# Two layers of a hybrid diffusion backbone: the scan's output split inside the scan's own program, responses in quarters of the TensorE array, rounding on ScalarE and merged rotations

## The chip, the cores and the metric

One core of one Trainium2 chip runs the whole program in one launch. The metric is device microseconds from the first to the last instruction, with what lies around them, as the median of several executions. Engine names are those of the profile: PE (TensorE matrix products), PEld (its weight loads), DVE (VectorE), ACT (ScalarE), POOL (GpSimd), SP (SyncE, whose only work here is issuing DMAs).

## What is computed

Input is a 1024-token latent stream and a 256-token context, both 1024 wide. Layer 0 runs two gated linear recurrences. Layer 1 runs windowed attention with 16 query heads and, beside it, an S5 state-space mixer; its output is what this case is about. All of it is computed in float32. The S5 half of layer 1, cut from the reference:

```python
for direction in range(2):
    abar = jnp.exp(lam * dt)
    bbar = ((abar - 1.0) / lam)[:, :, None] * bmat
    st_c = diag_scan(abar, order(einsum('blgh,gph->lbgp', uc, bbar)), None)
    st_l = order(diag_scan(abar, order(einsum('blgh,gph->lbgp', ul, bbar)), st_c[-1]))
    y_l = y_l + real(einsum('lbgp,ghp->blgh', st_l, cmat))
z = gelu(y_l)                      # then GLU: (z @ Wa) * sigmoid(z @ Wb) * silu(g_s5)
```

There are 64 channel groups of 16 channels, each with one complex diagonal state of size 64 in each direction.

## The kernel before

**Precision.** A matrix product in float32 accuracy is three products of fp32r halves: `mm3` (L67) issues high by high (L69), high by low (L70), low by high (L71). `split` (L63) makes the halves: the high one is a copy on ACT (L64), the low one a subtraction on DVE (L65). Small products of the S5 part run directly in f32; the trace shows each as two instructions. A f32 transpose is one.

**Layer 1 first stage (`layer1`, L904).** `main` (L932) projects the normed activations: eight units `u` (the S5 input), two `v`, two `k`, then 24 units `ga`, `gs`, `q`. A unit is one 128-column weight block (`g_fm`, L148): for each chunk of 512 tokens 24 matmuls into one of two PSUM banks, then an evacuation. That is 88 steps (yields) of `main`. `gs` units are passed through Silu (`silu`, L884) and stored to `gsD` (L971) in order of time.

**The scans' program (`S5.run`, L1427)** is a second generator that `weave` (L42) advances beside `main`: after step i of `main`, side steps are emitted until they stand in the ratio ns:nm to i (L975: 109 side steps to 83 main steps). It computes parameters (`params`, 11 steps), builds matrices for 16 groups-of-four (`build_a` L1469, `build_b` L1498) and runs 32 pairs of groups, three steps each:

- `table` (L1532): the rotation angles of a pair are rounded with two additions of a large constant (L1546, L1547, L1551, all DVE), then Sin on ACT (L1553, L1555). The scan's decays `dec` are written by ACT (L1545).
- `front_a` (L1561): input product on PE (L1576), evacuated on ACT to `sd`.
- `front_b` (L1585): rotate by the table (two products L1592, a subtraction L1593, an addition L1594), scan (L1595), rotate back (two products L1598, L1600, L1601), copy to `sx` (L1603, L1604 on ACT).
- `back` (L1606): output product on PE (L1614, L1616); after every fourth pair Gelu, and a store to `zF` (L1622).

In `build_a` the short responses are 8 products with a 128x128 block `g` as weights and 32 columns `kc` moving (L1490).

The tile framework takes the program's order as a priority and fixes each engine's queue when the kernel is built; within an engine, instructions then run in that order, each waiting for its inputs. SP's DMA queue is one such order: a DMA that waits for a buffer holds up those behind it. When a pool of tiles is closed, its memory goes to later pools, whose tiles wait for the last use of what lay there.

**The second stage.** After the weave, `g_glu` (L1029) loads z: for each of 8 channel blocks `cb`, eight loads into one of two buffers `zr` (L1037), then two splits (L1041) that turn the scans' order (t, n) into order of time (position 8n + 7 - t) with stride-8 access. Its tiles lie in the memory of pools that are closed after the weave. Then 16 units `b` and `a` of the GLU over two chunks of z (mm<-zh, whi), with `gsD` read back (L1053) and the result stored to `yT1` (L1056). `g_out` (L825) then multiplies this half by the output weights, adds the residual rows `x1` and stores partial rows `x2p` (`part`, L999). All of this is `main` (L989), woven with attention (`g_att`, L1072; scores L1131, softmax L1140 to L1151, products L1162 to L1171) at 46:150. The final `g_out` (L1025) does the attention half, block by block, reading `x2p`.

Of the kernel before, what the change touches and what calls it, by code (L numbers as in the profile page):

```python
# [9 lines left out]
F32 = mybir.dt.float32  # L10
# [8 lines left out]
D = 1024  # L19
# [35 lines left out]
class Body:  # L55
# [848 lines left out]
    def layer1(self):  # L904
# [8 lines left out]
        gaD = dram.tile([8, 128, 1024], F32, name="gaD")  # L913
        gsD = dram.tile([8, 128, 1024], F32, name="gsD")
        zF = dram.tile([64, 8, 16, 128], F32, name="zF")
# [12 lines left out]
        with tc.tile_pool(name="psum1", bufs=1, space=PSUM, reuse_waits="tile") as ps5:  # L928
            s5 = S5(self, left, ps5, uF, zF)
            nu = [0]  # L930

            def main():  # L932
# [28 lines left out]
                for kind, i in oB:  # L961
                    def ev(ps, c0, n):
                        lc = slice(c0 - 256, c0 - 256 + n)
                        if kind == "q":
                            self.rope(ps, c0, n, 0.125, [
                                qD[lc.start // 128:lc.stop // 128, i // 2, a * 32:a * 32 + 32,
                                   i % 2 * 2 + h].rearrange("b d t -> d b t")
                                for a in range(2) for h in range(2)])
                        else:
                            t = self.silu(ps, n)  # L970
                            self.nc.scalar.dma_start((gaD if kind == "ga" else gsD)[i, :, lc], t)  # L971
# [4 lines left out]
        left.close()  # L976
        self.right.close()
# [5 lines left out]
        with ExitStack() as low:  # L983
# [5 lines left out]
            def main():  # L989
                with tc.tile_pool(name="w1c", bufs=1, reuse_waits="tile") as wp, \  # L990
                        tc.tile_pool(name="zt", bufs=1, reuse_waits="tile") as zp:
                    st.end = len(st.order)
                    st.rawp, st.where = wp, lambda j: w1p if j % 2 == 0 else wp
                    yield from self.g_glu(zp, wp, zF, gsD)
                w1.close()
# [6 lines left out]
                yield from self.g_out(A["wo1"], self.yT1, 8, lat, lambda b: self.gl,  # L1002
                                      lambda b: self.x1[b * 128:b * 128 + 128], part, wp, b0=2, late=self.G)

# [23 lines left out]

    def g_glu(self, zp, wp, zF, gsD):  # L1029
        nc, V, S = self.nc, self.V, self.S  # L1030
        hz = [[zp.tile([128, 8, 512], F32R, name=f"z{x}{c}") for x in "hl"] + [c * 512, 512] for c in range(2)]
        st = self.st
        st.load(st.i + 1)
        for cb in range(8):
            t = zp.tile([128, 8, 128], F32, name="zr", tag="zr", bufs=2)
            for g in range(8):
                nc.sync.dma_start(t[g * 16:g * 16 + 16], zF[cb * 8 + g].rearrange("t h n -> h t n"))  # L1037
            t = t[:, ::-1].rearrange("p t n -> p n t")
            for zh, zl, c0, n in hz:
                h, lo = (x[:, cb].rearrange("p (n t) -> p n t", t=8) for x in (zh, zl))  # L1040
                self.split(h, lo, t[:, c0 // 8:(c0 + n) // 8])  # L1041
        yield
        for i in range(8):
            tb = {}

            def ev_b(ps, c0, n):
                t = tb[c0] = wp.tile([128, 512], F32, name="tb", tag="tb", bufs=3)
                S.activation(t, ps, AF.Tanh, scale=0.5)  # L1048

            def ev_a(ps, c0, n):  # L1050
                t = tb[c0]
                g = wp.tile([128, 512], F32, name="gsl", tag="gsl", bufs=2)
                nc.sync.dma_start(g, gsD[i, :, c0:c0 + n])  # L1053
# [192 lines left out]
class S5:  # L1246


    def __init__(self, K, left, ps, uF, zF):
        self.K, self.A, self.nc, self.left = K, K.A, K.nc, left  # L1250
        self.V, self.S, self.G, self.T = K.V, K.S, K.G, K.T
# [28 lines left out]
    def params(self):  # L1280
# [10 lines left out]
        self.exp(dt, raw[:, 2], n, r)  # L1291
        yield
        tt(wr, lre, dt, op=OP.mult)
# [53 lines left out]
        for t in range(2, 9):  # L1347
# [6 lines left out]
            tt(pw[:, 1, :, t], a, b, op=OP.add)  # L1354
        yield
        blk = self.wt("s5blk", (128, 16, 512), 1)
# [20 lines left out]
        stt(phl, dt, i2, phl, op0=OP.mult, op1=OP.add)  # L1377
        yield
        for x, y in ((wh, i1), (wh, i2), (dt, i1)):
# [29 lines left out]
        tt(out(0), out(0), t1, op=OP.subtract)  # L1409
        yield  # L1410
# [4 lines left out]
        yield  # L1415
        tt(out(4), cr, col(5), op=OP.mult)
# [10 lines left out]
    def run(self, nu):  # L1427

        nc, left, tile_pool = self.nc, self.left, self.K.tc.tile_pool
        par = left.enter_context(tile_pool(name="s5p", bufs=1, reuse_waits="tile"))  # L1430
        self.k5 = par.tile([128, 8, 64], F32, name="s5k5")
        self.nidx = par.tile([128, 320], F32, name="nidx")
        nc.sync.dma_start(self.nidx, self.A["nidx"])
# [18 lines left out]
        for p in range(32):  # L1452
# [11 lines left out]
            yield  # L1464
        self.back(todo.pop(0))

    steps = 11 + 2 + 96

    def build_a(self, c):  # L1469
# [23 lines left out]
        pv = pk[:, :128].rearrange("p (g d h) -> p d g h", g=4, d=2)  # L1493
        S.activation(kf[:, 1], pv[:, 1], AF.Copy)
# [37 lines left out]
    def table(self, p):  # L1532

        V, S = self.V, self.S
        ts, stt = V.tensor_scalar, V.scalar_tensor_tensor
        n, mask = self.nidx[:, :160], self.nidx[:, 160:]

# [6 lines left out]
        for g in range(2):  # L1544
            S.activation(dec[:, g], mask[:, None, :].to_broadcast([128, 2, 160]), AF.Copy, scale=col(2, g))  # L1545
# [39 lines left out]
    def front_b(self, q):  # L1585
# [3 lines left out]
        tab, dec = self.tabs.pop(q.p)  # L1589
        R, Q = self.wt("sr", (128, 2, 2, 160), 1), self.wt("sq", (128, 2, 2, 160), 2)  # L1590
        for o, i in ((R, 0), (Q, 1)):
            tt(o, q.D[:, i][:, :, None, :].to_broadcast([128, 2, 2, 160]), tab, op=OP.mult)  # L1592
        tt(R[:, :, 0], R[:, :, 0], Q[:, :, 1], op=OP.subtract)  # L1593
        tt(R[:, :, 1], R[:, :, 1], Q[:, :, 0], op=OP.add)  # L1594
        V.tensor_tensor_scan(*(x.rearrange("p a b n -> p (a b n)") for x in (Q, dec, R)), 0.0, op0=OP.mult, op1=OP.add)  # L1595
        U, W = R[:, :, :, 0:128], self.wt("sw", (128, 2, 2, 128), 1)
        for o, i in ((U, 0), (W, 1)):
            tt(o, Q[:, :, i, 31:159][:, :, None, :].to_broadcast([128, 2, 2, 128]), tab[:, :, :, 32:160], op=OP.mult)  # L1598
        Y = Q[:, :, :, 0:128]
        tt(Y[:, :, 0], U[:, :, 0], W[:, :, 1], op=OP.add)  # L1600
        tt(Y[:, :, 1], W[:, :, 0], U[:, :, 1], op=OP.subtract)  # L1601
        q.x = self.wt("sx", (128, 2, 2, 128), 3)
        S.activation(q.x[0:64], Y[0:64], AF.Copy)  # L1603
        S.activation(q.x[64:128], Y[64:128, :, :, ::-1], AF.Copy)  # L1604

# [48 lines left out]
def s5_host(f, A):  # L1654
# [17 lines left out]
    A["s5d"] = d  # L1672
    A["nidx"] = np.broadcast_to(np.concatenate([np.arange(160), np.arange(160) > 0]), (128, 320)).astype(np.float32)
    sh = np.zeros((128, 128), np.float32)
# [90 lines left out]
```

## Time and profile before

| what | value |
|---|---|
| median of 3 runs | 2752.55 us (2750.77 to 2753.32) |
| the profiled execution, its own time | 2755.79 us |
| its span, first to last instruction | 2754.0 us |
| mean granted clock of TensorE | 0.986 of full |
| busy: PE, PEld, DVE, ACT, POOL | 97%, 84%, 69%, 50%, 17% of the span |

Matmuls overlap, so PE's busy time is not its rate; the rate is read from the starts of successive matmuls in the timeline. A wait is put down to the engine whose instruction ended last before it. In the windows, "x57" counts instructions that run in a stretch, also those that only reach into it.

### The profile page before, as it was taken

The numbers are of one execution on the slowest core, as the hardware profiler recorded it, in microseconds if no ns is written. First come the engines' busy times: TensorE is split into PE (matmuls) and PEld (weight loads), VectorE is DVE, ScalarE is ACT, GpSimd is POOL, SyncE is SP. The second block draws the span as 40 slices with busy tenths as digits, with TensorE's granted clock in tenths as the row PEclk, the third lists the DMA queues.
The fourth block names the chain that finished last, engine by engine and source line by source line (L and its number), as shares of the span: only waits on it lengthen the run. The fifth ranks groups of instructions, "written<-read, shape, count | busy, mean of one in ns | idle before, by whom it ended". The sixth has DMA issues, their size and how long they took to land. (4 is left out here: it accounts for less than half of the span.)

```text
span 2754.0 us, 44850 instructions
## 1 busy us (share of the span) xinstructions
PE 2663.5 (97%) x15664; PEld 2300.3 (84%) x15664; DVE 1912.0 (69%) x5052; ACT 1381.4 (50%) x2907; POOL 456.9 (17%) x817
## 2 busy tenths in 40 slices
PE   6999999999999999998999999999999899999998
PEld 4998989888898888887887789888888688878887
DVE  5556655554565646637467679999996588899886
ACT  5545545434445435437233215666666455576552
POOL 1121120212212222223000000000000022225420
PEclk9999999999999999999999999999999899999999
DMA  6101011111110111123463445344443633243423
GB/s 241 33 24 60 26 49 41 49 54 51 56 57 31 57 56 41 53 65 108 134 208 127 161 129 127 101 133 108 117 110 115 178 89 107 89 146 121 133 97 128
DMA packets 231396, 262.24 MB, mean 95 GB/s; under 512 B 71105, under 2 KB 173761, under 8 KB 230913
## 3 DMA queue, kind: packets, MB, share of 16 engines
q1 hardware_dynamic: 178464, 223.97, 26.6%
q10 hardware_dynamic: 49696, 24.65, 3.2%
q0 software_dynamic: 3008, 10.75, 1.1%
q8 instruction: 124, 2.03, 0.3%
q14 instruction: 104, 0.84, 0.1%
HBM read 192.75 MB, written 66.52 MB: 94 GB/s over the span
## 5 line engine op out<-in xcount | busy, mean ns | idle before, releaser
L69 PE MATMUL mm<-hh,whi 128*128 128x512 f32 (+1 forms) x1800 | 671.7, 373 | 14.6 <-ACT gt L583 5.1
L71 PE MATMUL mm<-hh,wlo 128*128 128x512 f32 (+1 forms) x1800 | 667.9, 371 | 0.0
L70 PE MATMUL mm<-hl,whi 128*128 128x512 f32 (+1 forms) x1800 | 663.7, 369 | 0.5 <-DVE hl L65 0.5
L69 PEld LDWEIGHTS mm<-hh,whi 128*128 128x128 f32 x1800 | 341.1, 190 | 68.1 <-issue 6.2
L71 PEld LDWEIGHTS mm<-hh,wlo 128*128 128x128 f32 x1800 | 340.0, 189 | 53.3 <-issue 1.2
L70 PEld LDWEIGHTS mm<-hl,whi 128*128 128x128 f32 x1800 | 340.7, 189 | 52.3 <-DVE hl L65 1.2
L1151 POOL TENSOR_TENSOR P<-P,ast 128x640 f32<-128x640 f32 (+1 forms) x64 | 87.4, 1366 | 882.4 <-ACT tb L1048 635.9
L70 PE MATMUL mm<-owl,yh 128*128 128x512 f32 x576 | 226.9, 395 | 3.3 <-DVE owl L65 3.3
L69 PE MATMUL mm<-owh,yh 128*128 128x512 f32 x576 | 227.9, 396 | 0.7 <-ACT yh L64 0.7
L71 PE MATMUL mm<-owh,yl 128*128 128x512 f32 x576 | 226.2, 393 | 0.6 <-DVE yl L65 0.6
L65 DVE TENSOR_TENSOR wlo<-wraw,whi 128x1024 fp32r<-128x1024 f32 x117 | 146.5, 1252 | 97.5 <-ACT whi L64 97.4
L69 PE MATMUL mm<-whi,hh 128*128 128x256 f32 x720 | 205.5, 286 | 3.2 <-DVE v L364 3.2
L70 PE MATMUL mm<-wlo,hh 128*128 128x256 f32 x720 | 205.2, 285 | 0.0
L71 PE MATMUL mm<-whi,hl 128*128 128x256 f32 x720 | 202.8, 282 | 0.0
L563 DVE SCALAR_TENSOR_TENSOR S<-S,sc,st 128x128 f32<-128x128 f32 (+1 forms) x192 | 74.3, 387 | 161.8 <-PE st L558 161.3
L64 ACT ACTIVATE whi<-wraw 128x1024 fp32r<-128x1024 f32 x117 | 123.7, 1057 | 122.0 <-PE mm L70 93.2
L1145 ACT ACTIVATE P<-P,ast 128x640 f32<-128x640 f32 (+1 forms) x128 | 101.7, 796 | 77.7 <-DVE ast L1146 52.2
L69 PEld LDWEIGHTS mm<-whi,hh 128*128 128x128 f32 x720 | 135.6, 189 | 5.0 <-DVE v L364 4.1
L70 PEld LDWEIGHTS mm<-wlo,hh 128*128 128x128 f32 x720 | 135.9, 189 | 1.1
L71 PEld LDWEIGHTS mm<-whi,hl 128*128 128x128 f32 x720 | 135.6, 188 | 0.6
L70 PEld LDWEIGHTS mm<-owl,yh 128*128 128x128 f32 x576 | 108.5, 188 | 27.0 <-DVE owl L65 6.1
L69 PEld LDWEIGHTS mm<-owh,yh 128*128 128x128 f32 x576 | 108.5, 188 | 26.0 <-ACT ot L870 3.4
(400 smaller groups left out, 6170.0 us busy)
## 6 DMA issues: line engine op xcount, KB each, us to landing
wraw<-in_w SPq DMA_DIRECT2D x117, 512.0 KB, 3.6
yr<-yT SPq DMA_DIRECT2D x144, 128.0 KB, 2.7
owr<-in_wo SPq DMA_DIRECT2D x62, 256.0 KB, 5.6
whi<-in_wada SPq DMA_DIRECT2D x24, 512.0 KB, 3.5
adaw<-in_adaw SPq DMA_DIRECT2D x16, 512.0 KB, 10.2
qr<-qD SPq DMA_DIRECT2D x64, 128.0 KB, 2.7
yT<-gt SPq DMA_DIRECT2D x28, 256.0 KB, 2.3
x1p<-xr SPq DMA_DIRECT2D x10, 512.0 KB, 3.7
```

Of the source, the lines that this page charges most:

```text
L64: self.S.activation(hi, src, AF.Copy)
L65: (eng or self.V).tensor_tensor(lo, src, hi.bitcast(F32), op=OP.subtract)
L69: T.matmul(ps, sh, mh, start=first, stop=False)
L70: T.matmul(ps, sh, ml, start=False, stop=False)
L71: T.matmul(ps, sl, mh, start=False, stop=last)
L563: V.scalar_tensor_tensor(new, state[d], scal(d, b, 6, 7), pst[:, :dv], op0=OP.mult, op1=OP.add)
L1145: S.activation(p[:, j, :w], p[:, j, :w], AF.Exp, bias=nm[:, j:j + 1], accum_out=sm[:, j:j + 1])
L1151: G.tensor_tensor(p[:, 1, :w], p[:, 1, :w], es[:, 1:2].to_broadcast([128, w]), op=OP.mult)
```

## The change

- `gsD` is kept as [8, 128, 8, 128] in scan order; the Silu of `gs` reads PSUM with stride 8 and writes in scan order, and its store goes out in pieces of 64 numbers.
- z is no longer turned into order of time. The S5 pools are closed at the end of `S5.run`; a pool for z is opened there, and eight further side steps load each channel block and split it whole, 1024 contiguous columns at once. `g_glu` finds z ready and takes its small tiles from the pool `stg`.
- The residual rows are read and the partial rows written with a row stride of 8 (`rows`).
- `params` loses 5 yields; the weave's ratio becomes s5.steps + 9 = 113 to 86.
- `build_a`: `kc` becomes the weights (32 columns), `g` moves (128 columns), and the four products of one i go to four quarters of the array's columns; the result is copied by ACT and transposed.
- `table`: the first rounding (two L1546 and the L1547) becomes two ACT instructions of 160 columns and one of 320.
- `front_b`: two products of 640 become one of 1280, two of 512 one of 1024; buffers `sr`, `sq`, `sw` become `rq` (1) and `uw` (2); the scan's input is written over `sd`; `sx` goes from 3 buffers to 2.

```diff
+            def side():
+                yield from s5.run(nu)
+                zp = zx.enter_context(tc.tile_pool(name="zt", bufs=1, reuse_waits="tile"))
+                zh, zl = (zp.tile([128, 8, 1024], F32R, name=f"z{x}") for x in "hl")
+                hz.extend([zh[:, :, c:c + 512], zl[:, :, c:c + 512], c, 512] for c in (0, 512))
+                for cb in range(8):
+                    t = zp.tile([128, 1024], F32, name="zr", tag="zr", bufs=2)
+                    for g in range(8):
+                        nc.sync.dma_start(t[g * 16:g * 16 + 16].rearrange("h (t n) -> h t n", t=8),
+                                          zF[cb * 8 + g].rearrange("t h n -> h t n"))
+                    self.split(zh[:, cb], zl[:, cb], t)
+                    yield
...
+                            t = self.stg.tile([128, 8, 64], F32, name="sg", tag="sg", bufs=2)
+                            S.activation(t, ps.rearrange("p (n t) -> p t n", t=8)[:, ::-1], AF.Silu)
+                            self.nc.scalar.dma_start(gsD[i, :, :, lc.start // 8:lc.stop // 8], t)
...
-            weave(main(), s5.run(nu), 24 + 10 + 6 + 2 * len(oB) - 5, s5.steps)
+            weave(main(), side(), 24 + 10 + 6 + 2 * len(oB) - 2, s5.steps + 9)
...
+                def rows(x, b):
+                    return x[256:].rearrange("(n t) c -> t n c", t=8)[9 - b]
+
                 def part(b, x):
-                    nc.sync.dma_start(x2p[b * 128:b * 128 + 128], x)
+                    nc.sync.dma_start(rows(x2p, b), x)
...
-    steps = 11 + 2 + 96
+    steps = 6 + 2 + 96
...
-        for j in range(4):
-            for i in range(2):
-                T.matmul(pk[:, j * 32:j * 32 + 32], g[:, i, j].rearrange("p t h -> p (t h)"), kc[:, j, i],
+        for i in range(2):
+            for j in range(4):
+                T.matmul(pk[j * 32:j * 32 + 32, 0:128], kc[:, j, i], g[:, i, j].rearrange("p t h -> p (t h)"),
                          start=i == 0, stop=i == 1)
+        kq = self.wt("kq", (128, 128), 1)
+        S.activation(kq, pk[:, 0:128], AF.Copy)
+        T.transpose(pk[:, 128:256], kq, K.ident)
...
-            ts(r[:, g], n, col(7, g), MAG, op0=OP.mult, op1=OP.add)
-        ts(r, r, MAG, None, op0=OP.subtract)
+            S.activation(r[:, g], n, AF.Identity, scale=col(7, g), bias=mag)
+        S.activation(r, r, AF.Identity, bias=nmag)
...
+        RQ = self.wt("rq", sh, 1)
+        tt(RQ, D[:, :, :, None, :].to_broadcast(sh), tab[:, None].to_broadcast(sh), op=OP.mult)
+        tt(D[:, 0], RQ[:, 0, :, 0], RQ[:, 1, :, 1], op=OP.subtract)
+        tt(D[:, 1], RQ[:, 0, :, 1], RQ[:, 1, :, 0], op=OP.add)
+        Q = RQ[:, 0]
...
+        UW = self.wt("uw", sh, 2)
+        tt(UW, Q[:, :, :, None, 31:159].to_broadcast(sh), tab[:, None, :, :, 32:160].to_broadcast(sh), op=OP.mult)
```

## Rows read from the trace of the kernel before

**Rows 1.** The page, part 1: busy time, share of the span, instructions.
```profile
PE 2663.5 (97%) x15664; PEld 2300.3 (84%) x15664; DVE 1912.0 (69%) x5052; ACT 1381.4 (50%) x2907; POOL 456.9 (17%) x817
```

**Rows 2.** Windows: stretch, length, busy by engine (instructions), granted clock, DMA share, GB/s.
```profile
1752.00:2112.00 360.00, 358.52 (x1957) 309.49 (x1957) 348.49 (x626) 238.00 (x426) 0.00 (x0) 1.00 0.41 112
...
2129.64:2169.72 40.08, 25.92 (x57) 14.98 (x56) 19.25 (x20) 19.78 (x23) 0.00 (x0) 0.66 0.63 169
2169.72:2450.00 280.28, 279.33 (x1657) 246.72 (x1655) 229.34 (x655) 157.58 (x356) 58.33 (x50) 1.00 0.35 101
...
2600.00:2754.00 154.00, 140.18 (x737) 118.83 (x735) 120.39 (x354) 67.96 (x162) 27.92 (x24) 0.96 0.35 118
```

**Rows 3.** Waits of PE, 1640 to 2180 us: total, times, longest.
```profile
PE mm L69 <- ACT zh L64: 14.0, 12, 5.2
PE sb L1485 <- DVE G L1530: 3.8, 1, 3.8
```

**Rows 4.** The tile zr: duration ns min/median/max, first and last start.
```profile
L1037 SPq DMA_DIRECT2D zr<-zF x64: 302/428/709, 2112.0 to 2158.8; - x64
L64 ACT ACTIVATE zh<-zr x16: 1060/1074/1257, 2127.1 to 2162.8; 128x512 fp32r<-128x512 f32 x16
L65 DVE TENSOR_TENSOR zl<-zr,zh x16: 1044/1058/1159, 2128.3 to 2163.9; 128x512 fp32r<-128x512 f32 x16
...
DMA to landing us min/median/max: 2.1/2.6/4.6
```

**Rows 5.** PE's timeline (start, length): the scans' last output product; two projection matmuls.
```profile
2115.53 0.61 PE L1616 MATMUL yo<-sx,ct 128*128 128x128 f32 x4
...
2118.07 0.39 PE L69 MATMUL mm<-hh,whi 128*128 128x512 f32 x1
2118.30 0.39 PE L70 MATMUL mm<-hl,whi 128*128 128x512 f32 x1
```

**Rows 6.** DVE groups by form, 1640 to 2130 us: busy us, mean ns, idle before.
```profile
L1546 DVE TENSOR_SCALAR tb<-nidx,s5k 128x160 f32<-128x160 f32 x64 | 16.4, 299 | 9.4 <-DMA s5blk<-s5blk 9.3
...
L1547 DVE TENSOR_SCALAR tb<-tb 128x320 f32<-128x320 f32 x32 | 10.3, 323 | 0.3
```

**Rows 7.** DVE's timeline in the stage of the scans.
```profile
1837.14 0.83 DVE L1592 TENSOR_TENSOR sq<-sd,tab 128x640 f32<-128x640 f32 x1
1837.88 1.23 DVE L1528 TENSOR_TENSOR G<-bq 128x1024 f32<-128x1024 f32 x1
1839.01 0.69 DVE L1550 SCALAR_TENSOR_TENSOR tb<-nidx,s5k,tb 128x160 f32<-128x160 f32 x2
```

**Rows 8.** PE's timeline around the responses of one build.
```profile
1781.92 1.03 PE L1485 MATMUL sb<-cst,G 128*128 128x128 f32 x8
1782.79 1.87 PE L1490 MATMUL sk<-kc,G 128*128 128x32 f32 x16
1784.50 1.33 PE L1576 MATMUL pd<-ut,bt 128*128 128x160 f32 x8
```

**Rows 9.** PE's timeline in layer 0: four products with 32-column weights, one per quarter.
```profile
726.13 0.39 PE L70 MATMUL mm<-hl,whi 128*128 128x512 f32 x1
726.45 0.64 PE L225 MATMUL y<-whi,sc 128*32 128x256 f32 x8
727.02 0.51 PE L71 MATMUL mm<-hh,wlo 128*128 128x512 f32 x1
```

**Rows 10.** ACT groups by form, 1640 to 2130 us.
```profile
L64 ACT ACTIVATE whi<-wraw 128x1024 fp32r<-128x1024 f32 x30 | 31.8, 1058 | 23.5 <-PE mm L70 13.0 <-DVE G L1530 3.6 <-PE mm L71 3.3
...
L1553 ACT ACTIVATE tab<-tb 128x320 f32<-128x320 f32 x32 | 14.9, 466 | 9.0 <-DVE tb L1552 7.8 <-ACT sg L945 0.5 <-DVE kfb L1495 0.4
```

**Rows 11.** DMA issues: KB each, median us from issue to landing.
```profile
uF<-sg ACTq DMA_DIRECT2D x16, 256.0 KB, 3.1
```

**Rows 12.** The tile x2p: partial rows stored, first and last start.
```profile
L1000 SPq DMA_DIRECT2D x2p<-xr x8: 319/382/493, 2498.2 to 2633.3; - x8
```

**Rows 13.** DVE's timeline: the first addition onto x2p rows in the final product.
```profile
2644.77 0.69 DVE L873 TENSOR_TENSOR xr<-xr,ot 128x512 f32<-128x512 f32 x1
```

More of the change, by code (lines that the diff above doesn't have):

```diff
@@ L913, in layer1 @@
         gaD = dram.tile([8, 128, 1024], F32, name="gaD")
-        gsD = dram.tile([8, 128, 1024], F32, name="gsD")
+        gsD = dram.tile([8, 128, 8, 128], F32, name="gsD")
         zF = dram.tile([64, 8, 16, 128], F32, name="zF")
@@ L928, in layer1 @@
         with tc.tile_pool(name="psum1", bufs=1, space=PSUM, reuse_waits="tile") as ps5:
-            s5 = S5(self, left, ps5, uF, zF)
+            s5 = S5(self, ps5, uF, zF)
             nu = [0]
+            zx = ExitStack()
+            hz = []
+            def side():
[10 more added lines that the diff above has]
+                    yield
             def main():
@@ L989, in main @@
             def main():
-                with tc.tile_pool(name="w1c", bufs=1, reuse_waits="tile") as wp, \
-                        tc.tile_pool(name="zt", bufs=1, reuse_waits="tile") as zp:
+                with tc.tile_pool(name="w1c", bufs=1, reuse_waits="tile") as wp:
                     st.end = len(st.order)
                     st.rawp, st.where = wp, lambda j: w1p if j % 2 == 0 else wp
-                    yield from self.g_glu(zp, wp, zF, gsD)
-                w1.close()
+                    yield from self.g_glu(hz, gsD)
+                for x in (zx, left, w1):
+                    x.close()
                 wp = self.wp = low.enter_context(tc.tile_pool(name="ow1", bufs=1, reuse_waits="tile"))
                 self.gl = self.gate_bc(wp, 1, 0, "gbl")
+                def rows(x, b):
+                    return x[256:].rearrange("(n t) c -> t n c", t=8)[9 - b]
                 def part(b, x):
-                    nc.sync.dma_start(x2p[b * 128:b * 128 + 128], x)
-                yield from self.g_out(A["wo1"], self.yT1, 8, lat, lambda b: self.gl,
-                                      lambda b: self.x1[b * 128:b * 128 + 128], part, wp, b0=2, late=self.G)
+                    nc.sync.dma_start(rows(x2p, b), x)
+                yield from self.g_out(A["wo1"], self.yT1, 8, lat, lambda b: self.gl, lambda b: rows(self.x1, b),
+                                      part, wp, b0=2, late=self.G)
             att = self.g_att(ai, ap, pa, qD, kD, vD, gaD)
@@ L1027, in layer1, with g_glu @@
                 pass
-    def g_glu(self, zp, wp, zF, gsD):
+    def g_glu(self, hz, gsD):
         nc, V, S = self.nc, self.V, self.S
-        hz = [[zp.tile([128, 8, 512], F32R, name=f"z{x}{c}") for x in "hl"] + [c * 512, 512] for c in range(2)]
         st = self.st
         st.load(st.i + 1)
[L1034 to L1041, printed above, removed]
         yield
@@ L1046, in ev_b @@
             def ev_b(ps, c0, n):
-                t = tb[c0] = wp.tile([128, 512], F32, name="tb", tag="tb", bufs=3)
+                t = tb[c0] = self.stg.tile([128, 512], F32, name="rp", tag="rp", bufs=3)
                 S.activation(t, ps, AF.Tanh, scale=0.5)
@@ L1051, in ev_a @@
                 t = tb[c0]
-                g = wp.tile([128, 512], F32, name="gsl", tag="gsl", bufs=2)
-                nc.sync.dma_start(g, gsD[i, :, c0:c0 + n])
+                g = self.stg.tile([128, 512], F32, name="sg", tag="sg", bufs=2)
+                nc.sync.dma_start(g, gsD[i].rearrange("p t n -> p (t n)")[:, c0:c0 + n])
                 V.scalar_tensor_tensor(t, t, 1.0, ps, op0=OP.add, op1=OP.mult)
@@ L1246, with __init__ @@
 class S5:
-    def __init__(self, K, left, ps, uF, zF):
-        self.K, self.A, self.nc, self.left = K, K.A, K.nc, left
+    def __init__(self, K, ps, uF, zF):
+        self.K, self.A, self.nc = K, K.A, K.nc
         self.V, self.S, self.G, self.T = K.V, K.S, K.G, K.T
@@ L1291, in params @@
         self.exp(dt, raw[:, 2], n, r)
-        yield
         tt(wr, lre, dt, op=OP.mult)
@@ L1427, in run @@
     def run(self, nu):
-        nc, left, tile_pool = self.nc, self.left, self.K.tc.tile_pool
+        nc, left, tile_pool = self.nc, ExitStack(), self.K.tc.tile_pool
         par = left.enter_context(tile_pool(name="s5p", bufs=1, reuse_waits="tile"))
         self.k5 = par.tile([128, 8, 64], F32, name="s5k5")
-        self.nidx = par.tile([128, 320], F32, name="nidx")
+        self.nidx = par.tile([128, 322], F32, name="nidx")
         nc.sync.dma_start(self.nidx, self.A["nidx"])
@@ L1465, in run @@
         self.back(todo.pop(0))
-    steps = 11 + 2 + 96
+        left.close()
+    steps = 6 + 2 + 96
     def build_a(self, c):
@@ L1535, in table @@
         ts, stt = V.tensor_scalar, V.scalar_tensor_tensor
-        n, mask = self.nidx[:, :160], self.nidx[:, 160:]
+        n, mask, mag, nmag = (self.nidx[:, a:b] for a, b in ((0, 160), (160, 320), (320, 321), (321, 322)))
         def col(i, g):
@@ L1589, in front_b @@
         tab, dec = self.tabs.pop(q.p)
[L1590 to L1604, printed above, removed]
+        D = q.D
+        sh = [128, 2, 2, 2, 160]
+        RQ = self.wt("rq", sh, 1)
[3 more added lines that the diff above has]
+        Q = RQ[:, 0]
+        V.tensor_tensor_scan(*(x.rearrange("p a b n -> p (a b n)") for x in (Q, dec, D)), 0.0, op0=OP.mult, op1=OP.add)
+        sh = [128, 2, 2, 2, 128]
+        UW = self.wt("uw", sh, 2)
+        tt(UW, Q[:, :, :, None, 31:159].to_broadcast(sh), tab[:, None, :, :, 32:160].to_broadcast(sh), op=OP.mult)
+        U, W = UW[:, 0], UW[:, 1]
+        tt(U[:, :, 0], U[:, :, 0], W[:, :, 1], op=OP.add)
+        tt(U[:, :, 1], W[:, :, 0], U[:, :, 1], op=OP.subtract)
+        q.x = self.wt("sx", (128, 2, 2, 128), 2)
+        S.activation(q.x[0:64], U[0:64], AF.Copy)
+        S.activation(q.x[64:128], U[64:128, :, :, ::-1], AF.Copy)
     def back(self, q):
@@ L1672, in s5_host @@
     A["s5d"] = d
-    A["nidx"] = np.broadcast_to(np.concatenate([np.arange(160), np.arange(160) > 0]), (128, 320)).astype(np.float32)
+    A["nidx"] = np.broadcast_to(np.concatenate([np.arange(160), np.arange(160) > 0, [MAG, -MAG]]), (128, 322)).astype(np.float32)
     sh = np.zeros((128, 128), np.float32)
```

14 lines of the change are left out of this document (5 added, 9 removed).

## The prediction

> **What bounds the kernel now.** The page's first part comes first [rows 1]: PE is busy 97% of the span, so only two things can move the end: PE instructions that disappear, and stretches in which PE ran below its rate. The windows show where those are [rows 2]. In the stage of the scans (1752 to 2112 us) PE is busy 358.5 of 360 us, but DVE also 348.5: two engines are full at once. From 2129.64 to 2169.72 PE is busy only 25.9 of 40.1 us, at a granted clock of 0.66, and DVE and ACT are half idle. After that PE is full again to 2450; the tail from 2600 has 14 us of gaps. The waits name the hole: PE waited for ACT's high half of z, 12 times, 14.0 us in all [rows 3]. The tile zr tells why [rows 4]: 64 small loads start between 2112.0 and 2158.8 and the splits run behind them. They begin at 2112 because that is where the scans end: their last output product is at 2115.5 [rows 5].
>
> What the hole costs: 57 instructions run in it, of which one only reaches in, so 56 matmuls [rows 2]. At full clock one starts every 0.23 us [rows 5], so they need 12.9 us; the stretch lasted 40.1. **27.2 us are lost**, waiting and half clock together (1.2 GHz granted while PE was mostly waiting, 2.4 before and after).
>
> **Part 1, the responses.** The block of 16 instructions takes PE from 1782.79 to 1784.50, 1.71 us [rows 8]. Afterwards it has the same 16, with 32-column weights, 128 moving columns and four quarters. Before shows no such block in this stage, so I bound it: if the quarters ran one after another nothing is saved, 1.71; layer 0 has eight instructions of 256 columns over four quarters, as many columns in all, in 0.57 us, plus 0.09 that the step into them takes beyond the usual 0.23 [rows 9], together 0.66. I take 0.66, the nearer row in form. The added transpose is one instruction, 0.11 as those just before the block [rows 8], plus some 0.08 for a further switch of operands; call it 0.19. Saved: 1.71 - 0.66 - 0.19 = 0.86 us, in 16 builds **13.8 us** of a full PE. (End of the projections: 2129.6 becomes 2115.8.) The range of this term is -3 to +14.
>
> Rows 9 show that the step into the quarters costs 0.09 us. The Trainium skill, "TensorEngine Tiling (Array Packing)", section Tiling Modes, says that a change of tiling mode drains TensorE, which speaks against 16 such blocks between other matmuls, and its Theoretical Speedup gives up to four times for 32 columns. By four times and no drain the block would take 0.43 and the term would be 17.5 us; the trace agrees that there is a loss at the switch, and its 0.66 goes into the sum.
>
> **Part 2, the end of the scans.** Whether the hole closes depends on when the scans end, since z can't be split before. DVE sets that pace. Its instructions overlap by some 0.09 us: one of 640 elements, 0.83 long, is followed after 0.74, one of 1024, 1.23 long, after 1.13 [rows 7]; that is 1.02 ns an element, so 512 take some 0.61 and 1280 some 1.40. Per pair of groups DVE loses the first rounding, 2 x (0.299 - 0.09) + (0.323 - 0.09) = 0.65 us [rows 6], and the merges save 2 x 0.74 - 1.40 = 0.08 and 2 x 0.61 - 1.13 = 0.09. That is 0.82 us, in 32 pairs **26 us**. ACT takes the rounding: 0.47 for 320 columns [rows 10] and, by its half, some 0.3 each for 160, 1.1 us a pair, 35 us in all, with 16 copies of the responses some 4 more; ACT is busy 238 of 360 us [rows 2], so this lies beside. Should that cover fail, DVE waits for the table (rival 2). Dropping five side steps moves every later step 5/1.31 = 3.8 steps of the projection ahead, 22 us in the program's order; but DVE, not the order, held the scans back, so I count nothing for it beyond letting the 26 us be used. The scans then end at 2115.5 - 26 = 2090 or somewhat earlier.
>
> **Part 3, z.** Per channel block: 8 issues of 0.43 = 3.4 us, landing 2.6 [rows 4], one ACT copy 1.06 and one DVE subtraction 1.23 [rows 10, 7] in place of two strided ones each (1.07 and 1.06 each [rows 4]): 8.3 us. With two buffers two blocks pass per 8.3 us, so all eight take 4 x 8.3 + 3.4 = 37 us, from about 3 us before the last product: done at 2090 - 3 + 37 = 2124 at the latest. The GLU starts at 2115.8 and needs the eighth block after 7 x 3 x 0.23 = 4.8 us, at 2120.6. So most of the work lies beside the projections, and a stall of 0 to 4 us is left; I take 2, and up to 13 as its far end, if only half the DVE saving arrives and PE falls to its lower clock again. On SP these 64 loads now stand among weight loads; SP already waits for buffers in this stage and PE was still full [rows 2], so I count nothing; without that cover a late weight block stops PE at a unit's border. gsD's 16 stores go out in pieces like those of uF, which land after 3.1 us [rows 11]; nobody reads them before the GLU, so nothing.
>
> **Part 4, rows with stride 8.** Each partial row block now spreads over all the rows, so the final product's first read must wait for the last of 8 stores, at 2633.3 [rows 12]; with about 3 us for each transfer the rows are there at 2640. They are first added at 2644.8 [rows 13]. Nothing, at worst 6 us if yT1 loads queue behind that read on SP.
>
> **The sum.** 13.8 + 27.2 - 2 = 39 us. The one wait of DVE's making in this stage, 3.8 us [rows 3], and the slow clock after it may also go; I leave it out (0 to +8). The profiled execution took 2755.8 us, giving 2716.8; the median of the runs lies 3.2 below that execution, so **2714 us**.
>
> **Rivals.**
> 1. *The scans end too late.* If the scans end some 10 to 15 us later than 2090, z is done after the projections by as much and each late block stops PE, at half clock. For it: my margin is 4 us short even at 2090, and the scans' order is fixed ahead by a model of the times. Against: ending earlier in the program's order works the other way. Gain 14 + 27 - 17 to 22 = 19 to 24: about 2731.
> 2. *The rounding on ACT stalls DVE* (slower). Each table now goes ACT, DVE, ACT in place of DVE, ACT, and ACT runs in order behind evacuations. If DVE idles per pair for more than the 0.82 us saved, the scans end later than before. The hole stays, and z's 37 us follow: at 8 us later than now (1.07 us idle a pair) the gain of part 1 and of the shorter splits is used up; at 3 us a pair the scans end 70 us later and the time is some 2752 + 70 - 8 = 2815. Against: a table is made one pair ahead, and ACT has 34% to spare.
> 3. *More than I count.* The wait of rows 3 goes and the scans end well ahead, so the stall is 0: 2 + 6 to 8 more, about 2705.
> 4. *The quarters don't overlap here.* The term falls from 13.8 to -3, but the projections end later, so z is hidden: 2752.6 - 27 + 3 = about 2728.
>
> **How the numbers follow.** The forecast has 0.58 (2708 to 2722), rival 1 0.20, rival 3 0.09, rival 4 0.07, rival 2 0.06. The range 2700 to 2738 takes in all but rival 2 and some of rival 1 that is worse than worked out. A difference under 0.2%, some 5.5 us, can't be told from none. Faster 0.92; same 0.03, a rival 1 or 2 near its turning point; slower 0.05, rival 2.
>
> **What would show it.** Right: the last `yo` product some 25 us or more ahead of the last projection matmul; all zh splits before or within 5 us of the first mm<-zh; PE's waits for zh under 4 us; the granted clock at 1.00 there; L1490 in blocks of some 0.66 us; DVE under 95% in the scans' stage. Wrong: DVE idle before L1549 for ACT, DVE still full to the end of the projections, PE waiting for zh or whi, or xr holding up the final product.

## The result and the profile after

The changed kernel takes **2771.6 us** (median of 4 runs, 2769.7 to 2776.2), the kernel before 2752.9 in the same job: ratio **1.0069**, 95% interval 1.0052 to 1.0086. It is slower by some 19 us, where 39 us less were forecast, and lies outside the range (2700 to 2738).

The page's first part, the answer to [rows 1]:

```profile
PE 2656.1 (96%) x15680; PEld 2277.9 (82%) x15680; DVE 1883.9 (68%) x4884; ACT 1417.8 (51%) x3013; POOL 455.3 (16%) x817
```

PE has less to do (7 us less busy), and so has DVE (28 us less); ACT has 36 us more. The work went down as planned, and the span rose from 2754.0 to 2768.5: 14.5 us between the two profiled executions, 19 between the medians. The windows of the same stages (stretch, length, busy by engine with instructions, granted clock, DMA share, GB/s), for [rows 2]:

```profile
1752.00:2112.00 360.00, 347.71 (x1923) 290.32 (x1922) 316.02 (x478) 260.47 (x489) 0.00 (x0) 0.98 0.42 110
2112.00:2139.00 27.00, 27.00 (x141) 22.83 (x139) 15.35 (x22) 17.16 (x30) 0.00 (x0) 1.00 0.29 91
2139.00:2180.00 41.00, 22.75 (x48) 11.50 (x47) 10.69 (x9) 12.45 (x13) 0.00 (x0) 0.64 0.55 154
2180.00:2450.00 270.00, 269.15 (x1581) 237.16 (x1581) 222.25 (x625) 152.15 (x343) 56.79 (x48) 1.00 0.38 105
2600.00:2768.50 168.50, 156.71 (x835) 132.73 (x833) 134.48 (x392) 77.81 (x187) 38.08 (x31) 0.98 0.38 124
```

In the stage of the scans neither engine is full any more: DVE stands 44.0 of 360 us (11.5 before), PE 12.3 (1.5 before). The hole is still there, 10 us later: 41.0 us, 48 instructions that need 11.0 at one per 0.23, so 30 us lost against 27.2. PE's timeline shows the end of the scans and the step into the GLU, for [rows 5]:

```profile
2135.92 0.61 PE L1630 MATMUL yo<-sx,ct 128*128 128x128 f32 x4
...
2138.91 0.39 PE L71 MATMUL mm<-hh,wlo 128*128 128x512 f32 x1
2149.30 1.22 PE L69 MATMUL mm<-zh,whi 128*128 128x512 f32 x2 [10.00 <-ACT zh L64]
```

The scans end 20 us later than before (2115.53), the projections 9.5 later. From there to the end of the GLU it takes 6.2 us more (317.1 against 310.9), in all that follows 1.2 less: these are the 14.5 us. The tile zr, for [rows 4]:

```profile
L942 SPq DMA_DIRECT2D zr<-zF x64: 303/429/1107, 2139.8 to 2173.5; - x64
L64 ACT ACTIVATE zh<-zr x8: 1056/1056/1056, 2148.2 to 2176.8; 128x1024 fp32r<-128x1024 f32 x8
L65 DVE TENSOR_TENSOR zl<-zr,zh x8: 1224/1226/1226, 2149.3 to 2177.9; 128x1024 fp32r<-128x1024 f32 x8
```

z's own chain is what the prediction said, 39.3 us from the first load to the last subtraction's end (37 forecast); it begins 28 us later than in [rows 4]. Who kept DVE idle is in its waits, 1760 to 2140 us (total, times, longest):

```profile
DVE rq L1605 <- ACT tab L1567: 26.7, 14, 3.8
DVE wlo L65 <- ACT whi L64: 10.2, 6, 3.0
DVE G L1540 <- PE sk L1499: 3.4, 3, 3.1
DVE rq L1605 <- ACT sd L1594: 3.4, 1, 3.4
```

The first row stood at 1.5 us before. One such wait in ACT's and DVE's timelines:

```profile
1976.65 0.47 ACT L1565 ACTIVATE tab<-tb 128x320 f32<-128x320 f32 x1
...
1977.02 0.45 ACT L1566 ACTIVATE tb<-tb 128x320 f32<-128x320 f32 x1
1977.38 0.92 ACT L1558 ACTIVATE tb<-nidx,s5k 128x160 f32<-128x160 f32 x2
1978.32 1.28 ACT L1634 ACT_TABLE_LOAD   x1
1979.62 1.06 ACT L1634 ACTIVATE y<-y 128x1024 f32<-128x1024 f32 x1
1980.69 1.28 ACT L1567 ACT_TABLE_LOAD   x1
1981.99 0.56 ACT L1567 ACTIVATE tab<-tb,cst 128x320 f32<-128x320 f32 x1
```

```profile
1982.58 1.49 DVE L1605 TENSOR_TENSOR rq<-sd,tab 128x1280 f32<-128x1280 f32 x1 [2.48 <-ACT tab L1567]
```

Between the first Sin (L1565) and the second (L1567), on which DVE waits, ACT does the next table's rounding (L1558) and a Gelu with two loads of function tables (1.28 us each). This table's own rounding (L1559) had ended at 1967.86: from there to its use 14.7 us pass, about one pair's period (the 32 input products lie between 1674.6 and 2117.2, 14.3 us a pair). Over all 32 pairs the same distance is 9.9 to 30.2 us, 16.4 in the middle. By this reading nothing is left to absorb a delay; f2 below tests it.

### The profile page after: what moved, and what is told of

It reads as the page before. It is cut to its first block, busy times and chain, and to the rows that moved or that the text cites. A ratio compares the mean times of both kernels' runs of the same rounds, so it can differ in the third digit from the quotient of the medians.

```text
span 2768.5 us, 44797 instructions
## 1 busy us (share of the span) xinstructions
PE 2656.1 (96%) x15680; PEld 2277.9 (82%) x15680; DVE 1883.9 (68%) x4884; ACT 1417.8 (51%) x3013; POOL 455.3 (16%) x817
## 4 chain that ended last, share of the span: by engine, by line
PE 74%; DVE 12%; ACT 7%; DMA 4%; issue 3%; SPq 1%; ACTq 0%; POOL 0%; DVEq 0%; POOLq 0%
PE mm L69 18%; PE mm L70 18%; PE mm L71 18%; PE o L547 3%; PE st L558 2%; PE pt L1174 2%; PE att L518 2%; DVE tmp L448 2%; ACT L399 1%; PE pv L1183 1%; PE sc L1143 1%; PE pv L1182 1%; PE sc L1144 1%; PE pd L1588 1%; PE att L519 1%
```

## The experiments

All versions in one table. "Last yo" is the start of the scans' last output product, "proj" that of the last projection matmul, "GLU end" that of the last mm<-zh, "rest" the span's end minus that; these are read from each profile. The ratio is to the kernel before, run in the same job.

| version | median us | ratio, 95% interval | last yo | proj | GLU end | rest |
|---|---|---|---|---|---|---|
| before | 2752.9 | 1 | 2115.9 | 2129.4 | 2440.3 | 313.7 |
| after | 2771.6 | 1.0069 [1.0052, 1.0086] | 2136.3 | 2138.9 | 2456.0 | 312.5 |
| e1 after, rounding on DVE | 2760.7 | 1.0028 [1.0017, 1.0039] | 2117.9 | 2132.8 | 2438.1 | 321.5 |
| e2 before, rounding on ACT | 2767.6 | 1.0051 [1.0034, 1.0067] | 2123.6 | 2143.3 | 2446.5 | 320.3 |
| e3 before, quarters | 2764.5 | 1.0045 [1.0030, 1.0060] | 2130.0 | 2134.0 | 2451.0 | 315.3 |
| e4 before, z part | 2755.9 | 1.0010 [1.0000, 1.0019] | 2113.0 | 2128.0 | 2435.1 | 321.0 |
| f4 before, merged rotations | 2763.0 | 1.0032 [1.0019, 1.0045] | 2115.1 | 2137.0 | 2441.5 | 320.9 |
| f1 after, decays last | 2769.2 | 1.0054 [1.0039, 1.0069] | 2128.9 | 2150.7 | 2453.6 | 313.7 |
| f2 after, rounding ahead | 2743.0 | 0.9958 [0.9944, 0.9972] | 2095.7 | 2137.4 | 2429.2 | 315.1 |
| f3 after, side steps earlier | 2779.5 | 1.0090 [1.0075, 1.0105] | 2139.9 | 2140.2 | 2471.2 | 306.5 |
| g1 f2, old responses | 2734.8 | 0.9929 [0.9914, 0.9944] | 2086.8 | 2130.8 | 2423.6 | 309.4 |
| g2 f2, old rotations | 2754.3 | 1.0003 [0.9994, 1.0013] | 2110.7 | 2127.1 | 2433.6 | 317.4 |
| g3 f2, old z | 2751.1 | 0.9992 [0.9983, 1.0001] | 2107.1 | 2129.1 | 2431.3 | 319.9 |
| g4 f2, old params | 2742.8 | 0.9956 [0.9941, 0.9971] | 2092.8 | 2135.5 | 2425.3 | 315.6 |
| h1 f2, late quarters | 2742.6 | 0.9961 [0.9947, 0.9975] | 2097.0 | 2122.8 | 2420.5 | 321.3 |
| h2 before, late quarters | 2761.6 | 1.0028 [1.0018, 1.0039] | 2116.8 | 2122.9 | 2437.9 | 319.2 |
| h3 before, rounding ahead | 2756.0 | 1.0005 [0.9996, 1.0014] | 2106.9 | 2128.9 | 2428.4 | 321.9 |
| i1 before, other order | 2753.3 | 0.9997 [0.9987, 1.0006] | 2112.3 | 2127.3 | 2436.1 | 316.7 |
| i2 after, other order | 2776.7 | 1.0078 [1.0063, 1.0093] | 2137.7 | 2138.0 | 2468.0 | 308.4 |
| i3 g1, other order | 2744.5 | 0.9962 [0.9948, 0.9976] | 2084.0 | 2144.3 | 2429.5 | 313.2 |

### The parts one by one

e1: the rounding goes back to DVE in the changed kernel.

```diff
-            S.activation(r[:, g], n, AF.Identity, scale=col(7, g), bias=mag)
-        S.activation(r, r, AF.Identity, bias=nmag)
+            ts(r[:, g], n, col(7, g), MAG, op0=OP.mult, op1=OP.add)
+        ts(r, r, MAG, None, op0=OP.subtract)
```

> The changed kernel with the first rounding of the table back on DVE (two of 160 columns and one of 320 per pair); all else as changed. Theory A (the rounding on ACT makes DVE wait for the table, 26.7 us in the scans' stage, and that delays the scans): the last output product of the scans comes at 2115 or earlier instead of 2136, the 14 waits for the table go, time about 2740 (30 us less). Theory B (the merged rotations with fewer buffers delay the scans): DVE waits as before for something else, time stays within 5 us of 2771. Theory C (the new order of the steps in the program delays them): time stays at 2771.

The waits for the table fell to 7.3 us in 4 and the scans end 18 us earlier, at 2117.9, 3 us short of theory A. The GLU ends 17.9 us earlier too, but the rest takes 9.0 longer, so the time fell by 11, a third of the 30 expected. So the rounding is a cause of the late scans, and not of everything.

e2: the kernel before with that edit alone, reversed.

> The kernel before with only the first rounding moved to ACT. Theory A: DVE waits for the table 20 us or more in the scans' stage, scans end at 2130 to 2140, time 2765 to 2775. Theories B and C: DVE saves 0.65 us a pair, 21 us in all, the scans end at about 2095, time 2735 to 2745.

Waits and time (2767.6) come out as theory A says; the scans end 7.7 us later than before, at 2123.6, and not between 2130 and 2140. The DVE work that was saved is the same as in the change; it is lost in waits for the table, as this row of DVE's waits shows (1760 to 2140 us):

```profile
DVE sr L1592 <- ACT tab L1555: 24.8, 13, 2.9
```

e3: `build_a` alone taken from the change (products in quarters, copy `kq`, transpose).

> The kernel before with only the responses in quarters. The prediction's first term alone would give 14 us less, 2739. Against it: DVE sets the end of the scans (2115.5), which does not move, so the projections end 14 us earlier, the hole before the GLU grows by the same 14 us, and the time stays at 2753 (within 3).

Worse than either: the scans end 14 us *later* and the time rises by 12. PE, with less to do, stood longer: in its longest wait of the early builds (at 1744) 7.2 us for DVE's `G`, where it was 3.8 before [rows 3].

e4: the z part alone (side steps, gsD and rows; params with its 11 steps).

> The kernel before with the z part alone: z in scan order, its loads and splits as last side steps, the gate stored in scan order, rows with stride 8; scans, tables and responses as before. Theory C (order and z steps cost): 2765 or more. Theories A and B: the scans end as before (2115.5), z's shorter splits save some 3 us and the steps start a little earlier, 2745 to 2753.

The first stage gains as expected (last yo 2.9 us earlier, GLU end 5.2), but the rest takes 7 us longer and the time is 3 above. In its tail PE has a wait that before has not, a row of PE's waits (2600 to 2760):

```profile
PE mm L69 <- DVE rs L91: 2.2, 1, 2.2
```

The rows with stride 8 are not its cause: f4 below keeps the rows of before and has the same wait (PE's waits, 2600 to 2765).

```profile
PE mm L69 <- DVE rs L91: 2.9, 1, 2.9
```

f4: `front_b` alone (merged products, `rq`, `uw`, two `sx`).

> The kernel before with only the merged rotations and their buffers (rq one, uw two, scan input written over sd, sx two instead of three). By the prediction's term DVE saves 0.17 us a pair, 5.4 us, and the scans end at 2110: time 2748. Theory B (fewer buffers cost more than that): DVE or PE waits for sd, sx or rq grow by over 5 us, time 2760 or more. With the sums of the other single parts (+15 for the rounding, +12 for the quarters, +3 for z) against the whole change (+19), the merged rotations should show some -11: 2742.

The scans end 0.8 us earlier, not 5, and the time is 8 us above: neither -11 nor a growth of the waits named. Of the 8 us, 7.2 lie in the rest. At the last yo the four parts add up well: +7.7 +14.1 -2.9 -0.8 = 18, measured 20.4. They do not act each by itself, though: put into before, the rounding costs 7.7 us there (e2), taken out of the change it gives back 18.4 (e1). The quarters were not taken out of the change with the rounding left in its place, so how the two share the delay is not shown. The times (+15 +12 +3 +8) do not add up to the 19 of the whole.

### Mending the rounding

f1 moves the two writes of `dec` behind the Sin in `table`:

```diff
-            S.activation(dec[:, :, g], mask[:, None, :].to_broadcast([128, 2, 160]), AF.Copy, scale=col(2, g))
...
         S.activation(tab[:, :, 0], w, AF.Sin, scale=-TURN, bias=self.K.halfpi)
+        for g in range(2):
+            S.activation(dec[:, :, g], mask[:, None, :].to_broadcast([128, 2, 160]), AF.Copy, scale=col(2, g))
```

> The changed kernel with the two ACT writes of the decays moved to the end of the table's program, behind the roundings and the Sin. Theory A1 (the rounding stands behind the decays on ACT, which wait for the scan of the pair before, 19.6 us in 11 waits; so the table starts late): DVE's waits for the table fall from 26.7 us to 10 or less, the scans' last product comes some 15 us earlier (2120), time about 2757. Theory A2 (the chain over three engines is too long in itself): waits for the table stay over 20 us, time stays within 4 of 2771. Theory D (each change of the work makes the planner fix another order, whose waits are a matter of luck by some 10 us): any time between 2755 and 2780, with waits that change their kind.

The waits for the table stay at 24.4 us, though the scans end 7.4 us earlier: the decays in front of the rounding were not the reason (A1 falls). f2 makes the rounding one pair ahead, in a program of its own with its own tiles:

```diff
+    def rnd(self, p):
+        r = self.rs[p] = self.wt("tr", (128, 2, 160), 2)
+        for g in range(2):
+            S.activation(r[:, g], n, AF.Identity, scale=col(7, g), bias=mag)
+        S.activation(r, r, AF.Identity, bias=nmag)
...
                 self.table(p + 1)
+            if p < 30:
+                self.rnd(p + 2)
```

> The changed kernel with the rounding of ACT made one pair ahead, into a tile of its own (two buffers), so that DVE finds it ready. Theory A (1 or 2): DVE's 14.4 us of waits for the rounding go and those for the table fall to 10 or less, the scans end at 2115 or earlier, time 2740 to 2752. Theory D: 2755 to 2775, with other waits.

2743.0: **28.6 us less than the change, by moving three ACT instructions per pair to an earlier place.** ACT does the same work. (The earlier place needs a tile of its own with two buffers; the two come together in this edit.) In DVE's waits (1760 to 2140) the row of the table is gone; these are the first that belong to the scans:

```profile
DVE rq L1621 <- ACT sd L1610: 4.5, 4, 3.3
...
DVE tb L1565 <- ACT tb L1570: 1.0, 1, 1.0
```

The hole closes. In the stretch in which the change ran 48 PE instructions, f2 runs 171 (window as above):

```profile
2139.00:2180.00 41.00, 37.67 (x171) 30.87 (x172) 23.27 (x52) 18.53 (x31) 2.49 (x2) 0.96 0.99 232
```

z is split nearly in time too; the last block's subtraction starts at 2144.5, the GLU's products at 2139.4:

```profile
L65 DVE TENSOR_TENSOR zl<-zr,zh x8: 1224/1224/1226, 2106.1 to 2144.5; 128x1024 fp32r<-128x1024 f32 x8
```

h3 moves the rounding ahead in the kernel before, alone.

> The kernel before with only the first rounding moved to ACT, one pair ahead in tiles of its own. Theory A (not the work on ACT but the place of the rounding in the chain of a table made DVE wait): waits of DVE for the table under 8 us (24.8 with the rounding in the chain), scans end at about 2100, and the hole before the GLU shrinks; 2740 to 2747 against 2767.6. Rival (ACT is too full for it): waits stay over 15 us, 2760 or more.

Its mechanism is confirmed (no wait on the table's chain over 1.4 us, scans end 9 us earlier, GLU end 11.9 earlier); the time is not: the rest takes 8 us longer, and 2756.0 can't be told from before. Against e2, which does the same work with the rounding in its first place, h3 ends the GLU 18.1 us earlier and takes 11.6 us less, with the rest about the same (321.9 and 320.3).

f3 gives the side steps out faster:

```diff
-            weave(main(), side(), 24 + 10 + 6 + 2 * len(oB) - 2, s5.steps + 9)
+            weave(main(), side(), 24 + 10 + 6 + 2 * len(oB) - 14, s5.steps + 9)
```

> The changed kernel with the side steps given out faster (113 steps on 74 main steps instead of 86), so that all scans stand some 14% earlier in the program. If the place in the program's order sets the end of the scans: the last output product moves ahead by 15 us or more and the hole before the GLU closes in part, time 2750 or less. If ACT and DVE set it (theory A): the last product moves by less than 5 us, PE waits more inside the scans' stage, time within 6 of 2771.

The last product did not come earlier (2139.9, 3.6 us later): not the place in the program but the chain sets the end, as A says. The time rose by 8, as attention now stood in front of the GLU (PE waited 10.8 us for a `qa` of it).

### The version with the rounding ahead, part by part

Each takes back one part of the change's diff: g1 the responses (`build_a`), g2 the rotations (`front_b`), g3 z with rows, gsD and params, g4 the 11 steps of params.

> The version with the rounding of ACT one pair ahead (2743.0), with the responses as before the change (weights G, 32 columns). If the quarters are worth 0.86 us of PE in each of 16 builds once the scans no longer hold PE up: 14 us more, 2757. If a full DVE or a wait takes the gain in this setting too: within 4 of 2743.

> The version with the rounding ahead, with the rotations and buffers of before (four products, sr, sq, sw, three sx). DVE then has 5.4 us more; if DVE's work alone counts: the scans end some 5 us later (2101), still long before the projections end, time within 3 of 2743. If the fewer buffers of the merged form cost waits (PE waits for sx 8.0 us there): the waits for sx fall under 3 us and the time is some 5 us less, 2738.

> The version with the rounding ahead, with z as before the change (turned into order of time after the weave, rows and gsD as before, 11 steps of params). If the scans' end alone makes the hole: z's loads start at about 2100, the splits are done near 2150, 10 us after the projections; PE loses some 10 us there, 2750 to 2753. If the z steps inside the weave are worth nothing: within 4 of 2743.

> The version with the rounding ahead, with the 11 steps of params of before the change (side steps 22 us later in the program). If the five dropped steps cause the loss at 1740 to 1780 (15 us there: PE in order behind sx, kfb and sd that come late): the loss falls under 8 us and the time to about 2735. If not: the scans end 10 to 20 us later, still before the projections, time within 4 of 2743.

In this setting the merged rotations are worth 11 us and the z part 8, more than alone; the five steps of params nothing. The quarters cost 8 here too: without them 2734.8, **19 us below the kernel before**. None of the times written down for g1 and g2 came out. At the end of the GLU the rotations are worth 4.4 us and the z part 2.1, and the quarters cost 5.6; what is beyond lies in the rest. The two traces differ most around the fourth of the 16 builds. From the block of products to the product that needs its result (`sk<-kfb,shift`), with quarters (PE, ACT, PE, ACT, DVE, PE; a fence each for PE's and ACT's view):

```profile
1722.11 0.65 PE L1504 MATMUL sk<-G,kc 128*32 128x128 f32 x16
...
1729.73 0.27 PE L1508 MATMUL sk<-cst,kq 128*128 128x128 f32 x1
...
1736.97 0.33 PE L1521 MATMUL sk<-kfb,shift 128*128 128x64 f32 x2
```

```profile
1725.31 0.26 ACT L1507 ACTIVATE kq<-sk 128x128 f32<-128x128 f32 x1
...
1733.79 0.22 ACT L1511 ACTIVATE kfb<-sk 128x64 f32<-128x64 f32 x1
```

and with the old responses:

```profile
1718.64 1.87 PE L1503 MATMUL sk<-kc,G 128*128 128x32 f32 x16
...
1723.52 0.43 PE L1517 MATMUL sk<-kfb,shift 128*128 128x64 f32 x2
```

14.9 us against 4.9 (in the middle of the 16 builds 14.5 against 9.8): the copy and the transpose each queue behind other work (the transpose behind `pd`, the next copy behind a Gelu). In the change itself this build took 7.4 us (1715.57 to 1722.95), so the figure is not that of every order. PE then stands, as this window shows, first f2, then g1:

```profile
1740.00:1760.00 20.00, 12.13 (x70) 10.05 (x70) 20.00 (x32) 14.33 (x30) 0.00 (x0) 0.76 0.52 132
```

```profile
1740.00:1760.00 20.00, 20.00 (x130) 18.20 (x129) 19.60 (x33) 16.40 (x34) 0.00 (x0) 1.00 0.45 123
```

70 instructions against 130, at a granted clock of 0.76 against 1.00. The longest wait of f2 there is for a copy `sx` of the scans (4.7 us); that the early chain leads to it is argued, not shown.

h1 and h2 therefore use quarters from the third build on, on f2 and on before:

```diff
+        if c < 2:
+            for j in range(4):
+                for i in range(2):
+                    T.matmul(pk[:, j * 32:j * 32 + 32], g[:, i, j].rearrange("p t h -> p (t h)"), kc[:, j, i],
...
+        else:
```

> The version with the rounding ahead, with the responses as before the change in the first two builds and in quarters in the other 14. Theory K (the quarters cost time through the longer chain of the first builds alone: products, copy on ACT, transpose, copies; 17.3 us against 6.1 from the block at 1722 to the last kfb addition, and PE then stands at 1740 to 1780): the stall goes, PE keeps 14/16 of the saving, time 8 to 12 us below the version with the old responses (2734.8), about 2725. Rival L (the quarters cost in every build, by PE's switches of tiling or by the extra ACT and PE steps): time 2733 to 2743.

> The kernel before with quarters from the third build on. Theory K: the 12 us that all quarters cost there go; DVE still holds the scans, so PE's 12 us are lost at the hole before the GLU: 2750 to 2755. Rival L: 2760 to 2766.

Up to the end of the projections theory K holds: 8.0 us earlier than g1, 6.5 earlier than before, of the 12 that 14 builds were to save, and the delay of the scans is gone (2116.8 against 2130.0 in e3). In the total it doesn't show: both times lie in the ranges written down for rival L. h2 loses PE's gain at the hole, as forecast, its GLU ends 2.4 us earlier than before, and the rest takes 5.5 longer. h1 has lost 5 of its 8 us by the GLU's end, and then has this in its tail (PE's waits, 2690 to 2720):

```profile
PE mm L69 <- DVE ot L872: 5.5, 1, 5.5
```

so it ends 8 us behind g1. That quarters in the first two builds delay the projections' end is shown: by 14.6 us from h1 to f2 and 11.1 from h2 to e3; from 1740 to 1760 PE is full again in h1 (130 instructions, clock 1.00). By which chain is not: the fourth build, which keeps its quarters in h1, took 5.7 us there and 14.9 in f2, so those 14.9 were not the price of its own copy and transpose:

```profile
1719.78 0.64 PE L1512 MATMUL sk<-G,kc 128*32 128x128 f32 x16
...
1725.43 0.33 PE L1529 MATMUL sk<-kfb,shift 128*128 128x64 f32 x2
```

Whether late quarters are worth their 12 us in the end is open.

### The order by itself

i1, i2 and i3 change only the weave's ratio (main steps 82 for 83 in i1; 83 for 86 in i2 and i3, the same expression as in f3 with -5), so the work is the same and the order fixed by the planner another.

> The kernel before with the weave at 109 side steps to 82 main steps instead of 83: no work is changed, only the order that the planner fixes. Theory D (every new order is worth plus or minus some 8 us by itself): 2745 to 2762, away from 2753 by more than 3. If orders of the same work are worth the same: within 3 of 2753, and the costs of the single parts (+15, +12, +8, +3) are those of the parts.

> The changed kernel with the weave at 113 to 83 instead of 86. Theory D: 2762 to 2780, away from 2771 by more than 3; DVE's waits for the table stay over 20 us in any case, since they belong to the rounding's place and not to one order.

> The version with the rounding ahead and the old responses (2734.8), with the weave at 113 to 83 instead of 86. If its gain is that of the parts: 2729 to 2741 and the scans end some 40 us ahead of the projections again. If it was a lucky order: 2745 or more.

The shift is about 0, +5 and +10 us by the medians; by the ratios it is -1, +2 and +9, and i2's lies within its interval. i3's 2744.5 lies between the two ranges written down for it, just short of that of a lucky order. The scans' end stays put (2112.3, 2137.7, 2084.0) and so does the cause: i2 has 29.8 us of waits for the table. In i3 the projections end 13.5 us later than in g1, and PE waits up to 6.1 us for a weight split there. So a difference of under 10 us between two of these versions need not be the part's. Beyond it lie the rounding's place (28.6) and g1's distance to before, which is 11 to 19 us.

What the order does is seen in the column "rest". The traces give the order in which PE starts its 3280 matmuls behind the projections. It is the same, but for at most 21 places, within each of five sets of versions: before, e3 and f1 (rest 313.7, 315.3, 313.7); e2 and h3 (320.3, 321.9); e1 and h2 (321.5, 319.2); e4 and f4 (321.0, 320.9); f3 and i2 (306.5, 308.4). No two other versions agree in more than 2180 places. Within a set the rest differs by at most 2.3 us, over all by 15.4; f1 and before agree although the z part tells them apart. So the rest goes with the order of the products and not with the part that was changed; the 7 us that e4 and f4 lose there are of this kind, and e3's 12 us are not. The rest is not the same work everywhere either: in f3 and i2 only 1540 of PE's matmuls start behind the GLU's end, in the others 1618 to 1640, as more of the attention ran ahead of it.

## Why the prediction was wrong

**What bounds the kernel: right.** PE and DVE full in the scans' stage, the hole before the GLU set by the end of the scans: f2 closes the hole by ending the scans early (171 PE instructions against 48 in the same stretch).

**Part 1: the size right, its worth wrong.** The block takes 0.57 us plus 0.11 at the next matmul (1961.04, 1961.61, 1961.95 below), 0.68 where 0.66 was said, and the transpose 0.11 (0.19 said). That is 0.92 us a build, 14.7 in all. (Of the 0.19, the 0.08 came from no row.) Not the 13.8 us failed but the step from them to the end of the projections ("2129.6 becomes 2115.8"; measured 2138.9, and 2134.0 with the quarters alone): it left out that quarters in the first two builds make the scans later (2130.0 in e3, 2116.8 in h2), and that a freed PE waits for DVE. Rival 4 bounded the block's overlap, not its chain. The rows in question, from PE's timeline after, answer to [rows 8, 9]:

```profile
1961.04 0.64 PE L1499 MATMUL sk<-G,kc 128*32 128x128 f32 x16
1961.61 0.50 PE L71 MATMUL mm<-hh,wlo 128*128 128x512 f32 x1
1961.95 0.39 PE L69 MATMUL mm<-hh,whi 128*128 128x512 f32 x1
...
1966.52 0.27 PE L1503 MATMUL sk<-cst,kq 128*128 128x128 f32 x1
1966.55 0.48 PE L69 MATMUL mm<-hh,whi 128*128 128x512 f32 x1
1966.86 0.39 PE L70 MATMUL mm<-hl,whi 128*128 128x512 f32 x1
```

**Part 2: the step that failed**, at "ACT takes the rounding ... so this lies beside". It did not lie beside: DVE waited 26.7 us for the table, and the scans ended at 2136.3, not at 2090. The 1.1 us a pair on ACT were 1.48 (groups of ACT, 1640 to 2140: 47.3 us in all, where 35 were said):

```profile
L1558 ACT ACTIVATE tb<-nidx,s5k 128x160 f32<-128x160 f32 x64 | 29.6, 508 | 0.0
L1559 ACT ACTIVATE tb<-tb,nidx 128x320 f32<-128x320 f32 x32 | 17.7, 554 | 0.3
```

DVE's merged products last 1.49 and 1.23 us, followed after 1.41 and 1.13 as estimated from [rows 7]. ACT's free share was no cover, because the rounding stood at the head of a chain ACT, DVE, ACT, DVE in which each hop queues. Rival 2 named just this. Its price was asked in the right unit: 26.7 us over 32 pairs is 0.83 idle a pair, which cancels the 0.82 saved. But its arguments against, "a table is made one pair ahead" and "34% to spare", were taken as enough for a chance of 0.06; the chain took 14.7 us in the wait shown, so that one pair ahead was no slack. That DVE's waits only cancel its saving leaves the scans where they were; the 20 us by which they ended later are more than this term, and in e3 the quarters alone make 14.1.

**Part 3: void by its start, its chain right only behind the projections.** There it took 39.3 us for 37. With the scans early (f2) it ran among the projections' work and took 55.6 (2090.1 to 2145.7). The GLU begins 2.0 us after the projections there, the stall that was said, but PE's wait in it (1.6 us) is put down to the split of a weight, not to z.

**Part 4: right for the change.** The first read follows the last store of [rows 12] (2657.4 after 2654.2), and PE has no wait for it. The waits in the tails of e4 and h1 don't speak against it: e4's is in f4 too, without the stride; where h1's 5.5 us come from is open, and the range allowed for 6.

**The sum** has no term for the rest behind the GLU, which took 306 to 322 us over all versions by the order of its products. In the change itself this did not count: 312.5 against 313.7.

## What to carry to other kernels

Work moved to an engine with room is free only if its *place* is free: count the hops of the dependency chain, the queue at each, and compare with the period, before counting busy shares. When two engines are full together, relief of one alone need not help: e3 took some 14 us from PE alone and lost 12. Where a planner fixes the order, run the unchanged work in a second order first: its spread, here up to 10 us, is the least effect that a part's experiment can show. Versions whose traces show the same order can be compared more closely.

## What was not expected of the hardware

A transposition between matmuls delays the next one by only 0.03 us, and that one's successor by 0.08 more. A Gelu between two Sin costs ACT 3.67 us (1978.32 to 1981.99) for 1.06 us of work, two table loads included; it fell inside one of the waits above.
